# A hybrid DeltaNet / RWKV-7 step: the z projection of two segments moved out of the recurrence, with new pools, round order and job plan

## The chip, the cores and the metric

The kernel runs on one core of one Trainium2 chip. The metric is the device time of one execution in microseconds (us); lower is better. The kernel has five engines to schedule: TensorE (PE, matmuls; the load of a stationary operand is shown apart as PEld), VectorE (DVE), ScalarE (ACT), GpSimd (POOL) and SyncE (SP, which here issues every transfer).

## The reference

One step of a two-layer trunk over 1104 tokens: 64 sample tokens (8 sequences of 8) and 1040 prompt tokens (16 learned ones and 1024). Layer 0 is a gated DeltaNet and is not touched. Layer 1 is RWKV-7 time mixing. Cut to what the change touches:

```python
xx = xprev - xn
xs = xn[None] + xx[None] * mu[:, None, None, :]
rkvz = jnp.einsum('sbtd,sde->sbte', xs[:4], w_rkvz)      # four 1024x1024 projections
r, k, v, z = rkvz[0], rkvz[1], rkvz[2], rkvz[3]
...
def step(S, inp):                                         # per head of 64, 16 heads
    r_t, k_t, v_t, d_t, kk_t, b_t = inp
    S = (S * d_t[:, :, None, :]
         + jnp.einsum('bhvk,bhk->bhv', S, -kk_t)[..., None] * b_t[:, :, None, :]
         + v_t[..., None] * k_t[:, :, None, :])
    return S, jnp.einsum('bhvk,bhk->bhv', S, r_t)
...
y = (y - mean) * lax.rsqrt(var + GN_EPS) * lnx_w.reshape(H, N) + lnx_b.reshape(H, N)
y = y + jnp.sum(r_h * k_h * r_k, -1, keepdims=True) * v_h
y = y.reshape(B, T, D) * jax.nn.silu(z)
return y @ w_o, S, xn[:, -1]
```

After it come the residual add and a final RMSNorm.

## The kernel before

**Layout.** Activations lie with features on the partitions and tokens along the free axis. The tokens are cut into three segments (`SEGS`: 384, 384, 336). A product of a 1024-feature input with a 1024x1024 matrix is made in eight output tiles of 128 features; each fp32 product is three matmuls on split operands (high by high, low by high, high by low), so one output tile of one segment is 24 matmuls with 384 or 336 columns. `load_w` brings a tile's weights as two 256 KB transfers into `wraw` (two buffers) and splits them: ACT writes `whi`, POOL writes `wlo` (three buffers each).

**The dense stage of layer 1** (`layer1`). `keys_decay_rate` projects the keys and the decays. Then come the eight tiles of r (`todo` with m = 0) and the eight of v (m = 2), each over all three segments, by `project`. `mix` makes each projection's input from the normed activations `xb` into eight of eleven slots. Between the tiles stand five blocks of `rwkv_inverse`: each takes five (the last four) pair-segments through loads (`sld...`), a score product (`fL`), a chain of 31 steps on DVE (`inverse32`: `invtmp`, `invT`), a merge on PE (`mY`, `mU`) and a store of the result (`ttd`). They are started behind the tiles 1, 3, 5, 7 and 9. Then `mix_out` writes the mixed z input of segments 1 and 2 to HBM (`xzd`), and `gate_tiles` makes z of segment 0 (PSUM tile `dz`): per tile 24 matmuls, a tanh on ACT, a multiply on DVE and a store to `zd`. In this part a planner inside the framework orders every engine's instructions by its own simulated times, PE's too.

**The recurrence** (`wave`). There are 24 pair-segments: three segments by eight pairs of heads, each with six chunks of 64 tokens. The loop counts in half rounds `tau` from -3 to 53. Pair n starts at tau = 2n and makes one chunk each tau, so up to three pairs are in flight. `rwkv_front` prepares a pair (loads `fldcs`, `fldk`, `flda`, `fldr`, `fldv`; products on ACT, POOL and DVE) at tau = 2n - 3; its score products (`fG`), bonus (`fbonus`) and transposes (`fVT`, `fBT`) are dealt over the next two tau as `parts`. Each tau runs, for all pairs in flight:

1. `step_solve` and `step_scores` (matmuls into `rA`, then `X` on ACT),
2. `step_inner` (matmuls with `X`, then `UV` on ACT),
3. `step_state` (matmuls with `UV`, then the state `rS` on DVE).

Behind each of the three stages stand the parts, and then `fill`, which deals out dense work from a list `jobs`. At the end of the tau comes `step_outputs` (matmuls into `rA`, copied by ACT as `y`). PE's order is written out by hand here (`manual_schedule`); the planner orders the other engines. Two tau are one round, in which one pair begins and one ends. The end of a pair, `rwkv_finish`, normalises `y`, transposes it (`fyT`) and makes the operands `yh`, `yl` of the last product.

A job is a generator with a number of steps and a stretch of tau over which the steps are spread evenly; a step is six matmuls. The jobs before, in order: z of segment 1 (PSUM tile `zz`), the output product of segment 0 for pairs 0 to 3 (`project_out`, PSUM tile `zo`: eight tiles of 12 matmuls, added to `x1T` in HBM), the first half of z of segment 2, and so on; the final norms of segments 0 and 1 (`norms`: transposes `dfin`, then ACT, DVE, POOL) stand in the same list. `gates` reads its input back from `xzd`. The PSUM tiles of `zz` and `zo` have one buffer. Behind the loop come the output product of pairs 4 to 7 of segment 2 (96 matmuls into `d`) and the last norm.

**Pools.** Before the recurrence the pools of the dense stage are closed and `rwkv` and `fin` are opened from the right end of on-chip memory, where `xb` (8 tiles of 1113 floats, 35.6 KB per partition) lay outermost and the inverse's tiles further in. All of the recurrence's tiles are in `rwkv`, the masks and the states first.

Of the kernel before, what the change touches and what calls it, by code (L numbers as in the profile page):

```python
# [35 lines left out]
class Builder:  # L36
# [156 lines left out]
    def load_w(self, src, kt=8, into=None):  # L193
# [5 lines left out]
        for h in range(0, kt, 4):  # L199
            w = self.t(self.wp, [128, 4, 128], "wraw", 2)  # L200
            nc.sync.dma_start(w[:, :, 0:n], v[:, h:h + 4, :])
# [5 lines left out]
            self.split(w[:, :, 0:n], hi[:, :, 0:n], lo[:, :, 0:n], eng_lo="dve" if into else "pool")  # L207
# [800 lines left out]
    def mix(self, m, xb):  # L1008

        xs = [self.slots[(self.slot + k) % 11] for k in range(8)]  # L1010
        self.slot += 8
        for c0, n in SEGS:
# [4 lines left out]
    def mix_out(self, m, xb):  # L1017

        for k in range(8):
            for a, b in ((384, 768), (768, NT)):  # L1020
                x = self.mix_raw(m, k, a, b, xb[k], self.ev)
                self.nc.sync.dma_start(self.xzd[k][:, a:b], x)

    def gate_inputs(self, xa, s, pool, xb=None):

        nc, t = self.nc, self.t
        f = xa.rearrange("p k n -> p (k n)")[:, 0:6144].rearrange("p (x k n) -> p x k n", x=2, k=8)
        c0, n = SEGS[s]
        for k in range(8):
            if s == 0:  # L1030
                x = self.mix_raw(3, k, 0, n, xb[k], pool)
            else:
                x = t(pool, [128, 384], "zst", 2)[:, 0:n]
                nc.sync.dma_start(x, self.xzd[k][:, c0:c0 + n])
# [3 lines left out]
    def gate_tiles(self, x, s, ks, pool):  # L1038

        nc, t = self.nc, self.t  # L1040
        c0, n = SEGS[s]
        xh, xl = x
        load = lambda k: self.load_w(self.i["rwkv_w_rkvz"][0, 3][:, 128 * k:128 * k + 128])
        w = load(ks[0])
        yield
        for k in ks:
            w, w1 = load(k + 1) if k < ks[-1] else None, w
            p = self.ps("d", 4, "z") if s == 0 else self.ps("z", 1, "z")
# [8 lines left out]
            z = t(pool, [128, 384], "ev", 3) if s == 0 else t(pool, [128, 384], "zst", 2)  # L1057
            self.act(z[:, 0:n], p[:, 0:n], AF.Tanh, scale=0.5)
            nc.vector.scalar_tensor_tensor(z[:, 0:n], z[:, 0:n], 1.0, p[:, 0:n], op0=ALU.add, op1=ALU.mult)  # L1059
# [93 lines left out]
    def project(self, m, k, x, dst, apart=False):  # L1153
# [56 lines left out]
    def rwkv_masks(self, ap, first=False):  # L1210
# [22 lines left out]
        bones = t(ap, [128, 128], "pre", 3)  # L1233
# [12 lines left out]
    def rwkv_open(self):  # L1246
# [4 lines left out]
        self.xzd = self.dram([8, 128, NT], "xzd")  # L1251
# [79 lines left out]
    def rwkv_front(self, p, s):  # L1331

        nc, t, ap, col = self.nc, self.t, self.ap, self.pcol
# [11 lines left out]
        ld = self.rwkv_load(P.n, ap, "f", ("cs", "k", "a", "r", "v"))  # L1345
        kk, Dp, iD = self.rwkv_keys(p, ld, ap, "f")
        DC = P.DC = t(ap, [128, 14], "DC", NB + 2)
# [3 lines left out]
        AR = P.AR = t(ap, [128, 6, 2, 64], "AR", NB + 1)  # L1351
# [3 lines left out]
        k2 = t(ap, [128, 384], "k2", 1)  # L1355
# [4 lines left out]
        BK = t(ap, [128, 6, 2, 64], "BK", 2)  # L1360
# [4 lines left out]
        pr = t(ap, [128, 384], "pr", 1)  # L1365
        nc.vector.scalar_tensor_tensor(pr, ld["r"], pc("rwkv_r_k"), k2, op0=ALU.mult, op1=ALU.mult)
        ph, pl = t(ap, [128, 384], "prh", 1, F32R), t(ap, [128, 384], "prl", 1, F32R)
# [121 lines left out]
    def rwkv_finish(self, p, s, P):  # L1489
# [23 lines left out]
        t1 = t(ap, [128, 384], "k2", 1)  # L1513
# [68 lines left out]
    def project_out(self, s, yo, pairs, x2=None):  # L1582
# [6 lines left out]
        for ft in range(8):  # L1589
            if x2 is None:  # L1590
                x = t(self.fin, [128, 384], "zst", 2)
            elif len(x2) < 8:
                x = t(self.fin2, [128, 384], "x2", 8)
                x2.append(x)
            if x2 is None or pairs[0] == 0:
# [196 lines left out]
    def wave(self, xa, stay, last, pool):  # L1792
# [32 lines left out]
        def fill(now):  # L1825
            while jobs:
                f, k, a, b = jobs[0]
                if now < a:
                    return
# [75 lines left out]
```

## Time and profile before

| | us |
|---|---|
| three runs | 2449.97, 2446.77, 2454.0 (median 2449.97) |
| the profiled execution | 2446.91 |
| its span, first to last instruction of the program | 2445.1 |
| PE busy, share of the span | 2217.7, 91% |
| DVE, ACT, POOL busy | 1595.9, 1290.7, 1057.1 |
| mean granted clock of PE | 0.962 |

Positions are microseconds from the start of the span. The r projection starts at about 1472, the z tiles of segment 0 follow v at about 1770, and the first score product of the recurrence is at 1847.4. In a row of a stretch the columns are: the stretch, its length, then busy time and number of instructions of PE, PEld, DVE, ACT and POOL, the clock granted to PE as a share of full speed, the mean share of the DMA engines, and GB/s. In a row of waits stand who waited, for whom, the total, the number of times and the longest. Idle time of an engine that is not the bound costs nothing.

### The profile page before, as it was taken

The page shows a single profiled execution, that of the slowest core. Times are in us where ns is not written, and L with a number is a line of the kernel's source. Part 1 is how long each engine was busy: PE and PEld are TensorE (multiplying, and loading weights), DVE is VectorE, ACT ScalarE, POOL GpSimd, SP SyncE. Part 2 cuts the span into 40 slices and gives each one's busy share as a digit, 9 for nine tenths or more (in the row PEclk, how much of TensorE's full clock was granted, in tenths as well). Part 3 has the DMA queues.
Part 4 walks back from the last instruction along what each step waited for, and adds up shares of the span by engine and source line. Part 5 has one row for each costly group of instructions (what it writes and reads, how often), then busy time and mean ns, then how long its engine had stood idle before and what let it go on. Part 6 is the DMA issues. An engine that isn't in the chain of part 4 may idle for free. (4 is left out here: it accounts for less than half of the span.)

```text
span 2445.1 us, 54796 instructions
## 1 busy us (share of the span) xinstructions
PE 2217.7 (91%) x19737; PEld 1993.4 (82%) x19737; DVE 1595.9 (65%) x4193; ACT 1290.7 (53%) x3673; POOL 1057.1 (43%) x1454
## 2 busy tenths in 40 slices
PE   6989999999999999999999999988887898898887
PEld 5878989898888989889999998877775776777676
DVE  7878676876868595853357425698766675565554
ACT  5455555555656465564335557464334555555543
POOL 3435343433444344442314325453346556565534
PEclk9999999999999999999999999999987999999899
DMA  3323333333332424263441446767555345454542
GB/s 109 107 69 100 85 109 85 102 78 91 79 107 71 115 70 108 81 181 90 122 112 54 133 166 179 171 178 209 143 159 164 109 136 169 125 172 140 155 155 78
DMA packets 481546, 297.37 MB, mean 122 GB/s; under 512 B 188889, under 2 KB 466650, under 8 KB 481274
## 3 DMA queue, kind: packets, MB, share of 16 engines
q1 hardware_dynamic: 481274, 293.87, 42.7%
q8 instruction: 155, 2.54, 0.5%
q14 instruction: 117, 0.96, 0.1%
HBM read 206.30 MB, written 87.46 MB: 120 GB/s over the span
## 5 line engine op out<-in xcount | busy, mean ns | idle before, releaser
L90 POOL TENSOR_TENSOR wlo<-wraw,whi 128x512 fp32r<-128x512 f32 x260 | 346.1, 1333 | 418.6 <-ACT whi L86 392.2
L76 PE MATMUL d<-xc,whi 128*128 128x384 f32 (+3 forms) x846 | 236.5, 337 | 2.0 <-ACT ev L1160 2.0
L86 ACT CAST whi<-wraw 128x512 fp32r<-128x512 f32 x260 | 160.0, 616 | 138.6 <-PE dq L76 50.5
L410 DVE SCALAR_TENSOR_TENSOR cvy<-raw,cw,cvy 128x408 f32<-128x408 f32 (+2 forms) x288 | 178.0, 631 | 17.3 <-ACT cvy L62 15.4
L443 DVE TENSOR_TENSOR invtmp<-invA,invT 72x31 f32<-72x31 f32 (+31 forms) x403 | 164.5, 408 | 17.1 <-POOL invT L438 6.3
L445 DVE TENSOR_TENSOR invT<-invT,invtmp 72x31 f32<-72x31 f32 (+31 forms) x403 | 167.5, 416 | 6.3
L76 PEld LDWEIGHTS d<-xc,whi 128*128 128x128 f32 (+1 forms) x846 | 153.5, 188 | 9.6 <-issue 5.3
L76 PE MATMUL dz<-xc,whi 128*128 128x384 f32 (+1 forms) x480 | 149.3, 342 | 0.0
L76 PE MATMUL dv<-xc,whi 128*128 128x384 f32 (+1 forms) x480 | 146.8, 335 | 0.0
L76 PE MATMUL dz<-xa,whi 128*128 128x384 f32 (+1 forms) x416 | 141.1, 360 | 5.4 <-ACT whi L86 5.0
L76 PE MATMUL d<-xa,whi 128*128 128x384 f32 (+3 forms) x450 | 137.6, 339 | 3.4 <-ACT xa L86 2.5
L76 PE MATMUL d<-xc,wlo 128*128 128x384 f32 (+2 forms) x396 | 130.1, 338 | 0.0
L859 POOL TENSOR_SCALAR Sb<-Sb,eglb 128x128 f32<-128x128 f32 x128 | 79.6, 639 | 89.2 <-DMA Sb<-in_state_gdn 44.8
L76 PE MATMUL dv<-xa,whi 128*128 128x384 f32 (+1 forms) x288 | 99.9, 347 | 0.1
L76 PE MATMUL dz<-xa,wlo 128*128 128x384 f32 (+1 forms) x256 | 91.5, 358 | 0.9 <-POOL wlo L90 0.9
L76 PE MATMUL zz<-xa,whi 128*128 128x384 f32 (+1 forms) x256 | 84.8, 376 | 8.0 <-DVE zst L1059 8.0
L76 PEld LDWEIGHTS dz<-xc,whi 128*128 128x128 f32 x480 | 89.7, 192 | 0.8
L76 PEld LDWEIGHTS dz<-xa,whi 128*128 128x128 f32 x416 | 82.9, 201 | 8.6 <-ACT whi L86 6.8
L76 PEld LDWEIGHTS d<-xa,whi 128*128 128x128 f32 (+1 forms) x450 | 82.5, 188 | 8.3 <-ACT xa L86 2.8
L76 PEld LDWEIGHTS dv<-xc,whi 128*128 128x128 f32 x480 | 88.5, 188 | 0.5 <-issue 0.4
L76 PE MATMUL d<-xa,wlo 128*128 128x384 f32 (+3 forms) x252 | 85.1, 338 | 0.9 <-POOL wlo L90 0.9
L62 ACT ACTIVATE o<-rA,gcol 128x128 f32<-128x128 f32 x128 | 46.6, 371 | 74.5 <-DVE S L770 74.1
(512 smaller groups left out, 7119.7 us busy)
## 6 DMA issues: line engine op xcount, KB each, us to landing
wraw<-in_gdn_w_in SPq DMA_DIRECT2D x96, 256.0 KB
wraw<-in_rwkv_w_rkvz SPq DMA_DIRECT2D x96, 256.0 KB
Sb<-in_state_gdn SPq DMA_DIRECT2D x64, 256.0 KB
wraw<-in_rwkv_w_o SPq DMA_DIRECT2D x48, 256.0 KB
E<-drow SPq DMA_DIRECT2D x24, 384.0 KB
attn<-drow SPq DMA_DIRECT2D x24, 384.0 KB
wraw<-in_gdn_w_out SPq DMA_DIRECT2D x36, 256.0 KB
out_s_gdn<-Sb SPq DMA_DIRECT2D x32, 256.0 KB
```

The lines of the kernel that those rows point to most:

```text
L62: return self.nc.scalar.activation(out, in_, func, bias=bias, scale=scale, **kw)
L76: self.nc.tensor.matmul(out, lhsT, rhs, start=start, stop=stop)
L86: nc.scalar.copy(hi, x)
L90: e.tensor_tensor(lo, x, hi.bitcast(F32), op=ALU.subtract)
L410: nc.vector.scalar_tensor_tensor(y[:, 0:wd], raw[:, k:k + wd], cw[k], y[:, 0:wd], op0=ALU.mult, op1=ALU.add)
L443: nc.vector.tensor_tensor(tmp, A[:, j, j + 1:32].unsqueeze(2).broadcast_to([nb, n, m]), Tv[:, j, 0:m].unsqueeze(1).broadcast_to([nb, n, m] ...
L445: nc.vector.tensor_tensor(Tv[:, j + 1:32, 0:m], Tv[:, j + 1:32, 0:m], tmp, op=ALU.subtract)
L859: nc.gpsimd.tensor_scalar(Sb[:, u], Sb[:, u], self.eglb[:, hv, 4 * g + u:4 * g + u + 1], None, op0=ALU.mult)
```

## The change

- z of segments 0 and 1 becomes a third projection in the dense stage (`todo` has m = 3): `mix` puts its input in eight slots, and `project` makes two segments from each weight tile, with the tanh and the multiply (`gate`) where r and v have a copy. `mix_out` and the HBM buffer `xzd` go. The slots are given by a table.
- The input of segment 2 is made in the dense stage behind the first z tile (`gate_inputs` at n = 16), and only z of segment 2 is a job of the recurrence.
- The inverses start behind the tiles 1, 4, 7, 10 and 13 of 24.
- Pools: `front` (the tiles of `rwkv_front`) is opened first from the right, then `system` (masks, states, `UV`, `rTT`), then `rwkv` and `fin`.
- Round order: `step_outputs` follows `step_state` at once, and `fill` stands behind the second and the third stage, ahead of the parts; behind the first stage there is none.
- The job list: z of segment 2 over tau -2.5 to 14, then four output products of eight tau each with the PSUM tiles `z` (one buffer) and `d` (two) in turn, then segment 2. The norms are in a second list that runs beside it.
- The last product: pairs 4 to 6 over tau 52.1 to 54, and pair 7 alone behind the loop (24 matmuls). `load_w` takes fewer than four rows of tiles.

```diff
-        todo = [(m, k) for m in (0, 2) for k in range(8)]
+        todo = [(m, k) for m in (0, 2, 3) for k in range(8)]
+        slots = {0: (0, 1, 2, 3, 4, 5, 9, 10), 2: (6, 7, 8, 0, 1, 2, 9, 10), 3: range(3, 11)}
         for n, (m, k) in enumerate(todo):
             if k == 0:
-                x = self.mix(m, xb)
-            self.project(m, k, x, {0: self.rd, 2: self.vd}[m], k in range(8))
-            if n in (1, 3, 5, 7, 9):
-                self.rwkv_inverse((1, 3, 5, 7, 9).index(n), ip)
-        self.mix_out(3, xb)
-        for _ in self.gate_tiles(self.gate_inputs(xa, 0, self.ev, xb), 0, range(8), self.ev):
-            pass
+                x = self.mix(m, xb, slots[m], SEGS[0:2] if m == 3 else SEGS)
+            self.project(m, k, x, {0: self.rd, 2: self.vd, 3: self.zd}[m], k in range(8))
+            if n in (1, 4, 7, 10, 13):
+                self.rwkv_inverse((1, 4, 7, 10, 13).index(n), ip)
+            if n == 16:
+                zin = self.gate_inputs(xa, xb)
...
-        self.ap = rpool("rwkv", ctx)
-        fp = self.fin = rpool("fin", ctx)
-        self.rwkv_masks(self.ap)
-        t, ap = self.t, self.ap
+        self.fp, ap = rpool("front", ctx), rpool("system", ctx)
+        t, self.ap = self.t, rpool("rwkv", ctx)
+        self.fin = rpool("fin", ctx)
+        self.rwkv_masks(ap)
...
     def project(self, m, k, x, dst, apart=False):
...
-        ps = (self.dense(w, 128, *x, s, bufs=4) for s in range(3)) if apart else self.dense3(w, 128, *x)
+        ps = (self.dense(w, 128, *x, s, bufs=4) for s in range(2 if m == 3 else 3)) if apart else self.dense3(w, 128, *x)
         for (c0, n), p in zip(SEGS, ps):
             f = t(self.ev, [128, 384], "ev", 3)
-            nc.scalar.copy(f[:, 0:n], p[:, 0:n])
+            if m == 3:
+                self.gate(f[:, 0:n], p[:, 0:n])
+            else:
+                nc.scalar.copy(f[:, 0:n], p[:, 0:n])
             nc.sync.dma_start(dst[k][:, c0:c0 + n], f[:, 0:n])
...
-        ld = self.rwkv_load(P.n, ap, "f", ("cs", "k", "a", "r", "v"))
+        ld = self.rwkv_load(P.n, fp, "f", ("cs", "k", "a", "r", "v"))
     (and kk, Dp, iD, DC, AR, k2, BK, pr, prh, prl in fp likewise)
...
-            p = self.ps("z", 1, "o") if pairs[0] == 0 or s < 2 else self.ps("d", 2)
+            p = self.ps(*tag, "o")
...
-        jobs = [(lambda: gates(1, range(8)), 33, -3, 14), (lambda: out(0, 0), 17, 14, 19), (lambda: gates(2, range(4)), 20, 19, 24.5),
-                (lambda: out(0, 4), 17, 24.5, 30), (lambda: out(1, 0), 17, 30, 35), (lambda: gates(2, range(4, 8)), 17, 35, 40),
-                (lambda: norms(0), 11, 40, 41), (lambda: out(1, 4), 17, 41, 45), (lambda: norms(1), 11, 45, 47),
-                (lambda: out(2, 0, x2), 17, 47, 53.9), (lambda: out(2, 4, x2), 17, 54.1, 55), (lambda: self.finish(2, x2), 6, 55, 56)]
+        jobs = [(gates, 33, -2.5, 14), (lambda: out(0, 0, 4, Z), 17, 14, 22), (lambda: out(0, 4, 8, DD), 17, 22, 30),
+                (lambda: out(1, 0, 4, Z), 17, 30, 38), (lambda: out(1, 4, 8, DD), 17, 38, 46),
+                (lambda: out(2, 0, 4, Z), 17, 46, 51), (lambda: out(2, 4, 7, DD, x2), 17, 52.1, 54),
+                (lambda: out(2, 7, 8, DD, x2), 9, 54.1, 55), (lambda: self.finish(2, x2), 4, 55, 56)]
+
+        more = [(lambda: norms(0), 5, 31, 36), (lambda: norms(1), 5, 47, 51), (lambda: x2.extend(self.sums_in(2)) or iter(()), 1, 51.6, 52)]
...
-            stages = (self.step_solve, self.step_scores), (self.step_inner,), (self.step_state,)
+            stages = (self.step_solve, self.step_scores), (self.step_inner,), (self.step_state, self.step_outputs)
             for g in range(3):
                 for f in stages[g]:
                     for x in items:
                         f(*x)
+                if g:
+                    fill(tau + g / 2)
                 for f in parts[g]:
                     f()
...
-                fill(tau + (g + 1) / 3)
-            for x in items:
-                self.step_outputs(*x)
```

More of the change, by code (lines that the diff above doesn't have):

```diff
@@ L1006, in rwkv_norm, with mix @@
                 nc.sync.dma_start(self.o["p_rwkv_shift"][0][:, c], lr[9 * k + 8:9 * k + 9])
[L1008 to L1012, printed above, removed]
+    def mix(self, m, xb, slots, segs=SEGS):
+        xs = [self.slots[k] for k in slots]
+        for c0, n in segs:
             for k in range(8):
@@ L1331, in rwkv_front @@
     def rwkv_front(self, p, s):
-        nc, t, ap, col = self.nc, self.t, self.ap, self.pcol
+        nc, t, ap, fp, col = self.nc, self.t, self.ap, self.fp, self.pcol
         P = Ctx()
@@ L1648, in finish @@
                     nc.sync.dma_start(yp[128 * tt - 80:128 * tt - 80 + nr, hs], y[0:nr])
-            for _ in range(3 if s < 2 else 1):
-                yield
+            yield
     def build(self):
@@ L1786, in layer1 @@
         with tc.manual_schedule(engines={mybir.EngineType.PE}):
-            self.wave(xa, stay, last, pool)
+            self.wave(zin, stay, last, pool)
         last.close()
@@ L1790, in layer1, with wave, gates @@
         self.psum.close()
[L1792 removed]
+    def wave(self, zin, stay, last, pool):
         nc, t = self.nc, self.t
         P, x2 = {}, []
[L1798 to L1813 removed]
+        Z, DD = ("z", 1), ("d", 2)
+        out = lambda s, a, b, tag, x=None: self.project_out(s, [P[8 * s + q].out for q in range(a, b)], range(a, b), tag, x)
+        def gates():
+            yield from self.gate_tiles(zin)
+            stay.close()
+            self.fin2 = pool("fin2", last)
+            self.fw = t(self.fin2, [128, D], "fw")
+            nc.sync.dma_start(self.fw, self.i["final_norm_w"].rearrange("(o d) -> o d", o=1).broadcast_to([128, D]))
+        def norms(s):
             x = self.sums_in(s)
```

112 lines of the change are left out of this document (44 added, 68 removed).

## The prediction

> **What bounds the kernel now.** I read the page first (who is busy, where the clock drops), then the stretches of layer 1 one by one, then PE's waits in each of them, then the chain that ended last.
>
> ```profile
> PE 2217.7 (91%) x19737; PEld 1993.4 (82%) x19737; DVE 1595.9 (65%) x4193; ACT 1290.7 (53%) x3673; POOL 1057.1 (43%) x1454
> PEclk9999999999999999999999999999987999999899
> ```
>
> PE is the busiest by far, and its clock dips at three quarters of the span, where the dense stage of layer 1 hands over to the recurrence. So the question is what PE does per stretch. I cut layer 1 at the start of the recurrence (1847.4) and at the transposes `fyT` of pairs 0, 3, 19 and 22, that is at the ends of tau 7, 13, 45 and 51:
>
> ```profile
> 1472.00:1770.00 298.00, 269.24 (x2572) 233.50 (x2571) 224.16 (x484) 162.61 (x351) 124.52 (x191) 0.97 0.67 176
> 1770.00:1847.40 77.40, 52.85 (x546) 45.54 (x545) 51.28 (x100) 30.15 (x63) 38.54 (x61) 0.79 0.64 178
> 1847.40:1941.80 94.40, 84.22 (x897) 68.71 (x897) 53.70 (x141) 48.72 (x129) 54.33 (x74) 0.89 0.43 124
> 1941.80:2004.00 62.20, 55.14 (x773) 44.16 (x771) 43.83 (x129) 35.16 (x105) 34.75 (x42) 1.00 0.46 128
> 2004.00:2366.10 362.10, 311.65 (x3863) 261.76 (x3859) 204.04 (x600) 200.90 (x623) 202.35 (x220) 0.93 0.51 151
> 2366.10:2404.80 38.70, 33.49 (x447) 27.31 (x445) 21.57 (x80) 17.72 (x64) 19.14 (x19) 0.99 0.37 111
> 2404.80:2445.10 40.30, 24.63 (x197) 22.64 (x194) 17.36 (x42) 10.38 (x25) 16.80 (x16) 0.92 0.26 81
> ```
>
> In these rows no other engine is above 76% of a stretch, and PE's idle time (length less busy) plus what the low clock costs is the whole room: idle 28.8 + 24.6 + 10.2 + 7.1 + 50.5 + 5.2 + 15.7 = 142 us, and the clock (1 less its share, times the length) 9 + 16 + 10 + 0 + 25 + 0 + 3 = 63 us. The change adds and removes hardly any matmul; it can only win or lose in these 200 us.
>
> **The change part by part.**
>
> The price of a matmul: in a stretch where PE never stops,
>
> ```profile
> 1400.00:1450.00 50.00, 50.00 (x301) 50.00 (x300) 11.27 (x12) 21.82 (x42) 9.66 (x11) 1.00 0.48 167
> ```
>
> 301 of them take 50 us, 0.166 us each at full clock. Now the fill, one row of tile `zz`, then two of tile `zo`:
>
> ```profile
> 2004.00:2366.10 362.10, 40.42 (x192) 32.76 (x192) 3.98 (x8) 3.58 (x8) 0.93 0.51 151
> 2004.00:2366.10 362.10, 85.63 (x384) 67.18 (x384) 17.59 (x32) 0.93 0.51 151
> 2366.10:2404.80 38.70, 14.30 (x72) 10.97 (x72) 2.68 (x6) 0.99 0.37 111
> ```
>
> *z moved.* 192 matmuls of segment 1 go from the recurrence to the dense stage: 192 x 0.166 = 32 us off the one, 32 us onto the other. z of segment 2 takes the place that segment 1 had at the start (same steps per tau), so the 192 of tau 14 to 45 are what vanishes from the recurrence. With the tile go 8 weight tiles less (16 transfers, 16 casts on ACT, 16 subtractions on POOL) and 32 transfers of `xzd`; none was on PE's path except in the handover, so I cost them at nothing there. The mixing of z is the same 24 pieces as before; the tanh and multiply of eight more tiles come to the dense stage beside 8.0 us of PE work per weight tile.
>
> *Dense stage, r and v (298 us).* Same PE work. The inverses start every 3 tiles in place of every 2. PE's waits here are theirs:
>
> ```profile
> PE fL L76 <- DVE skk L1305: 10.2, 10, 2.6
> PE fbpp L73 <- DMA invR<-rssd: 7.0, 3, 3.3
> ```
>
> DVE is at 224 of 298 us, so a thinner stream should lose less; the slots 9 and 10, read last by the keys, may cost r's first tile 1 to 2 us. I take -5, between -15 and +15.
>
> *Handover (77.4 us).* Now:
>
> ```profile
> PE fG L76 <- POOL fDp L1270: 13.6, 1, 13.6
> PE dz L76 <- ACT whi L86: 5.0, 6, 1.7
> 1830.22 1.17 PE L76 MATMUL mU<-sTT,invY 32*32 32x32 f32 x24 [0.43 <-DMA sTT<-r_u]
> 1834.06 0.32 SPq L1328 DMA_DIRECT2D ttd<-sTT  x1
> 1836.98 0.50 SPq L1261 DMA_DIRECT2D fldcs<-csd  x1
> 1847.44 1.65 PE L76 MATMUL fG<-AR,BK 64*128 64x128 f32 x12 [13.64 <-POOL fDp L1270]
> ```
>
> The last inverse stores its result at 1834.06; only 2.9 us later the first load of the recurrence (`fldcs`) is issued, SP's queue having stood before that behind weights and z input; then loads, ACT, POOL and DVE of one whole front run before `fG`, with PE idle for 13.64 us. After the change the front's tiles (seven loads and three keys of 1.5 KB, AR 15.4, BK 6.1 and the rest, 43 KB a partition) lie mostly on the 35.6 KB of `xb`, whose last reader is the input of segment 2 behind the first of eight z tiles. So the first fronts can run under seven tiles of z, and one weight tile now feeds 48 matmuls (8.0 us) where it fed 24 (4.0 us), against 5.0 us of weight waits now. The new stretch is 384 x 0.166 = 64 us for z, the rest of the inverses' matmuls (546 - 186 = 360, at 1.17 us per 24 at half clock, so 0.024 each at full: 9 us), and 5 for stops: 78 us, +1. Bounds: 73 with no stop, 96 if the whole hole and the weight waits stay. What would be late next is the last inverse: it starts behind tile 13, about 1472 + 14/16 x 295 = 1730, and its PE work stands ahead of the recurrence. I count on it ending inside the z tiles.
>
> *Tau -2 to 13 (94.4 + 62.2 us).* Same fill. The first stretch now starts with a cold clock (0.89 of 94.4 us: 10 us lost) and 10 us idle; with fronts ready and PE coming straight from z I take half: -9 (0 to -15), and -2 for the next.
>
> *Tau 14 to 45 (362.1 us, sixteen rounds of 22.6).* The first and the last of three quiet rounds, then the `zo` work of the first, then PE's waits over the stretch:
>
> ```profile
> 2139.60:2159.30 19.70, 18.30 (x241) 15.37 (x239) 12.18 (x37) 12.21 (x38) 12.64 (x14) 1.00 0.60 173
> 2179.30:2198.80 19.50, 18.05 (x243) 15.28 (x239) 12.27 (x37) 11.92 (x38) 12.68 (x14) 1.00 0.58 169
> 2139.60:2159.30 19.70, 7.81 (x36) 6.09 (x36) 1.60 (x4) 1.00 0.60 173
> PE rA L80 <- ACT y L1487: 12.5, 15, 1.7
> PE zo L76 <- DVE zst L1610: 11.9, 9, 2.5
> PE dfin L73 <- DVE f2k L1643: 7.9, 3, 3.6
> PE zz L76 <- DVE zst L1059: 7.2, 4, 3.4
> PE fG L76 <- DVE k L1514: 1.1, 1, 1.1
> ```
>
> A quiet round is 19.7 us with 36 fill matmuls and PE busy 18.1. After the change four output products of 96 are spread over these sixteen rounds: 24 a round. 19.7 - 12 x 0.166 = 17.7. The wait for `y` goes, since `step_outputs` now has fill and parts behind it before its PSUM tile is wanted: 12.5 us over 16 rounds, but not all of it in quiet ones, so -0.5: 17.2 a round. The 22.6 of today is the quiet round plus bursts: up to 48 fill matmuls in a round, two steps on a one-buffer tile in a row (the waits on `zst`), the norms' eleven steps in one tau (`dfin`), and the low clock behind each. In the new list a one-buffer tile has about five us between its steps, and the norms take five tau. So 16 x 17.2 = 275, plus 8 for sample rows and the 48 `dfin` transposes, plus 10 for stops that I can't place: 293, -69. Bounds: PE's bare work, (18.1 - 2.0) x 16 + 8 = 266; and all of today's stops kept, 362 - 32 = 330.
>
> Three waits could take the place of those removed. `X` now has only the score products between `step_scores` and `step_inner`:
>
> ```profile
> 2161.24 0.72 ACT L62 ACTIVATE X<-rA,rk 128x64 f32<-128x64 f32 x3 [1.46 <-PE rA L80]
> 2161.35 1.10 PE L76 MATMUL fG<-AR,BK 64*128 64x128 f32 x12
> ```
>
> All three `X` end at 2161.96, the score products at 2162.45: covered, so I cost it at nothing; if ACT is late with them by the length of one of its other instructions in half of the tau, that is 0.3 us a tau, 10 us, inside the bounds. `UV` and `rS` keep a fill step and a part ahead of their readers. On SP the norms' `x1T` loads now stand among the weights of the running product; at five tau apiece they have time.
>
> *Tau 46 to 51.* 96 fill matmuls in place of 72, 24 x 0.161 = +4, norms(1) there too, less stops: +4.
>
> *The end (40.3 us).* The transpose of pair 23, then the chain that ended last:
>
> ```profile
> 2412.20 0.92 PE L76 MATMUL fyT<-ident,y 64*64 64x64 f32 x24 [1.69 <-POOL y L1507]
> 2415.87 6.12 PE d L76 x38
> 2423.34 2.83 DMA wraw<-in_rwkv_w_o
> 2426.27 0.63 ACT whi L86
> 2426.97 1.29 POOL wlo L90
> 2430.70 0.67 PE dfin L73 x4
> ```
>
> 38 matmuls in 6.12 us are 0.161 each. Now pair 23's output waits 7.4 us (2404.8 to 2412.2), 96 matmuls and stops take 17.5, the last norm 15. After: 72 matmuls (11.6) stand ahead of the transpose of pair 23, then about 3 us of DVE, ACT and POOL for `yh` and `yl` with nothing on PE to cover them, then 24 matmuls (3.9) fed by eight small weight tiles through two `wraw` buffers. A 256 KB tile now takes 2.83 + 0.63 + 1.29 us from transfer to `wlo`; a quarter of it I put at 2.7, 1.35 per tile with two buffers, so some 7 us. Then 15. Together 11.6 + 1 + 3 + 7 + 15 = 38 with no stop; I take 41, +1 (-3 to +6).
>
> Sum: -5 + 1 - 9 - 2 - 69 + 4 + 1 = -79 on the profiled span of 2445.1: 2366. That execution was 2446.91, 1.8 above its span, and 3.1 below the median 2449.97; so 2366 + 5 = 2371.
>
> On the clock, the row of the handover has 0.79 over 77.4 us, 16 us lost around one hole of 13.6. The Trainium skill, "TensorE: Matmul & The Clock Gate", section "What's actually happening", says PE falls to half rate after an idle window of about 3.4 us and comes back after one busy window; that hole would then cost 1.7 us and not 16, and waits under 3.4 us nothing. By that rule the clock's share of my gain in tau 14 to 45 would be near zero and the sum some 15 us worse; the row of that stretch (0.93 of 362 us, 25 us lost, with longest waits of 3.6 us) speaks against taking it so strictly.
>
> **The rivals.**
>
> *The rounds are paced by DVE and POOL, not by PE.* In the quiet rounds each is busy 12.2 to 12.7 of 19.7 us, and a front is a chain over ACT, POOL and DVE on single buffers. For it: VectorE's products with POOL beside them are stretched,
>
> ```profile
> L1366 DVE SCALAR_TENSOR_TENSOR pr<-fldr,pcol,k x24: 604/636/1616, 1845.2 to 2325.9; 128x384 f32<-128x384 f32 x24
> ```
>
> 0.60 us at best and 1.62 at worst, and shorter rounds put more of them beside each other. Against it: PE's waits for the front in tau 14 to 45 are 1.1 us in all (`fG`). If it holds, rounds stay at 19.5: 16 x 2.3 = 37 us more, 2408. The Trainium skill, "GPSIMD Engine Reference", section "1. Specifications", says that POOL shares VectorE's ports to on-chip memory when VectorE has two inputs there, which fits the row; it does not say how much.
>
> *The hole stays.* The pools do not do what the layout allows: the last inverse, started later, or SP's queue holds the first front to the end of z. Then 13.6 us idle and the cold start (8) come back: 2393.
>
> *Slower: the recurrence does not shorten at all.* The dense stage takes its 32 us for z of segment 1, while a round is a latency chain (state to solve to inner to state) that fill only pads, so that less fill is only more idle time. Then 2450 + 32 = 2482 less the handover's gain of up to 20. Its point: a round of tau 14 to 45 must fall from 22.6 by 2.0 us to pay for the 32 us; at over 20.6 the change loses. Against it:
>
> ```profile
> 2381.00:2393.40 12.40, 5.96 (x30) 4.57 (x30) 1.13 (x3) 1.00 0.24 68
> ```
>
> Two tau with two pairs in flight and 30 fill matmuls took 12.4 us, so the chain is no longer than about 6 us a tau, against 8.6 forecast.
>
> **How the numbers follow.** Forecast (2335 to 2400): 0.64. Paced by DVE and POOL (about 2408): 0.13. The hole stays, or the stops of today stay in part, up to 2430: 0.12. The recurrence does not shorten: 0.07. Between them, within 0.3% (7 us, about what three runs can tell from no change): 0.04. The range takes in the first two and the better half of the third, 2335 to 2425: the low end is -79 with the bounds of the recurrence (266 for 293) and a little of the dense stage; the high end is the stops kept (330 for 293) with the hole half kept. Faster 0.89, same 0.04, slower 0.07.
>
> **What would show it.** Right: `fG` follows the last z matmul of the dense stage within 3 us, near 1848; the rounds of tau 14 to 45 are near 17 to 18 us with PE over 90% busy; the wait of `rA` for `y` is gone from PE's list; the stretch after the last round is about as long as now. Wrong: a wait of `rA` on `X` of some us in all, `fG` waiting for the front, PE waiting for `mU` of the last inverse at the end of z, or the last weight tiles late by more than 10 us.

## The result, and the profile after

| | before | after |
|---|---|---|
| median of the runs | 2448.37 us | 2420.19 us (2414.01 to 2422.7) |
| ratio to before | | 0.9878, 95% interval 0.9851 to 0.9905 |
| profiled execution | 2446.91, span 2445.1 | 2422.7, span 2421.0 |

The kernel is 28 us faster in the medians and 24 in the profiled pair. The forecast was 79: the sign was right, the size was not. The page's row of PE, its clock, and then the stretches of layer 1 (columns as before), cut at the first `fG` and at `fyT` of pairs 0, 3, 19 and 22:

```profile
PE 2213.4 (91%) x19737; PEld 2003.7 (83%) x19737; DVE 1620.5 (67%) x4201; ACT 1279.8 (53%) x3665; POOL 1049.8 (43%) x1446
PEclk9999999999999999999999999999998999999998
```

```profile
1472.00:1770.00 298.00, 273.69 (x2532) 237.35 (x2531) 220.32 (x471) 162.09 (x351) 127.15 (x195) 0.95 0.64 164
1770.00:1860.50 90.50, 80.30 (x776) 74.80 (x774) 61.50 (x124) 38.37 (x81) 43.93 (x62) 0.94 0.49 142
1860.50:1957.60 97.10, 81.55 (x897) 68.55 (x899) 57.86 (x148) 47.65 (x128) 54.78 (x74) 0.91 0.46 131
1957.60:2026.80 69.20, 58.30 (x785) 49.06 (x782) 47.62 (x130) 34.83 (x106) 37.75 (x44) 0.93 0.41 115
2026.80:2329.40 302.60, 269.23 (x3659) 232.20 (x3653) 211.99 (x583) 180.26 (x582) 178.38 (x199) 0.97 0.52 155
2329.40:2377.90 48.50, 39.78 (x484) 32.57 (x483) 25.55 (x83) 21.56 (x72) 22.90 (x23) 1.00 0.52 163
2377.90:2421.00 43.10, 25.33 (x174) 21.81 (x170) 18.71 (x47) 10.65 (x30) 15.15 (x21) 0.84 0.26 80
```

| stretch | before | forecast | after | miss |
|---|---|---|---|---|
| r, v, handover, to the first `fG` | 375.4 | 371 | 388.5 | +17 |
| up to tau 7 | 94.4 | 85 | 97.1 | +12 |
| tau 8 to 13 | 62.2 | 60 | 69.2 | +9 |
| tau 14 to 45 | 362.1 | 293 | 302.6 | +9.5 |
| tau 46 to 51 | 38.7 | 43 | 48.5 | +6 |
| end | 40.3 | 41 | 43.1 | +2 |

Six misses of one sign add up to 55 us (79 less the 24 of this pair); the rounds did shorten from 22.6 to 18.9 us. A first clue is in the page: DVE is busy 25 us longer than before, with eight instructions more. PE's waits in tau 14 to 45:

```profile
PE rA L80 <- ACT X L62: 15.9, 11, 1.6
PE rA L80 <- DVE rS L1470: 12.7, 29, 2.2
PE rA L80 <- ACT y L1481: 2.4, 5, 1.4
```

The waits on `zst` and `dfin` are gone and `y` is down from 12.5. In their place stand two that I had costed at nothing: `X`, and `rS`. Here is one place of the first, from the timeline (start, length, instruction, idle time before it and what ended it):

```profile
2142.51 1.69 DVE L1509 SCALAR_TENSOR_TENSOR lz<-k,lnb,lz 128x384 f32<-128x384 f32 x1
...
2142.53 1.26 POOL L90 TENSOR_TENSOR wlo<-wraw,whi 128x512 fp32r<-128x512 f32 x1
...
2142.41 0.52 ACT L62 ACTIVATE X<-rA,rk 128x64 f32<-128x64 f32 x2 [1.33 <-PE rA L80]
2144.24 0.51 ACT L86 CAST yh<-lz 128x384 fp32r<-128x384 f32 x1 [1.31 <-DVE lz L1509]
2144.66 0.70 ACT L62 ACTIVATE k<-flda,omka,pcol 128x384 f32<-128x384 f32 x1
2145.27 0.29 ACT L62 ACTIVATE X<-rA,rk 128x64 f32<-128x64 f32 x1
...
2145.62 0.45 PE L80 MATMUL rA<-X,rTT 128*64 128x64 f32 x4 [1.54 <-ACT X L62]
```

Two `X` are made at once. The third stands in ScalarE's queue behind `yh` and `k`, and both wait for VectorE's `lz`: `yh` reads it, and `k` writes the tile `k2`, in which `lz` still reads the first product of the finished pair. `lz` itself takes 1.69 us, with POOL's `wlo` beside it to 2143.79. In 13 of the 16 rounds `lz` takes 1.4 us or more, and there it ends about 0.4 us behind a POOL instruction that started with it (`wlo` in 12 of them); in the other three `wlo` had ended 0.05 us after the start of `lz`, and `lz` took about 0.6. The group of `lz` in tau 14 to 45 (ns, least, median and most), first before, then after:

```profile
L1515 DVE SCALAR_TENSOR_TENSOR lz<-k,lnb,lz x16: 546/616/687, 2006.3 to 2345.3; 128x384 f32<-128x384 f32 x13, 128x336 f32<-128x336 f32 x3
```

```profile
L1509 DVE SCALAR_TENSOR_TENSOR lz<-k,lnb,lz x16: 556/1692/1698, 2028.8 to 2315.0; 128x384 f32<-128x384 f32 x13, 128x336 f32<-128x336 f32 x3
```

The Trainium skill, "SBUF — State Buffer", section "Who interferes with whom", says that a VectorE instruction with two inputs in on-chip memory contends with a POOL instruction that reads it, for a port pair that is an exclusive lock, and that the order of issue decides who blocks. The trace fits: `lz` ends 0.41 us behind `wlo`, at 2144.20, as if it had waited for it. Their starts are 0.02 us apart, so which was issued first can't be read here.

### The profile page after: what moved, and what is told of

It is laid out like the page before. It is cut to its first block, busy times and chain, and to the rows that moved or that the text cites. A ratio compares the mean times of both kernels' runs of the same rounds, so it can differ in the third digit from the quotient of the medians.

```text
span 2421.0 us, 54809 instructions
## 1 busy us (share of the span) xinstructions
PE 2213.4 (91%) x19737; PEld 2003.7 (83%) x19737; DVE 1620.5 (67%) x4201; ACT 1279.8 (53%) x3665; POOL 1049.8 (43%) x1446
## 5 line engine op out<-in xcount | busy, mean ns | idle before, releaser
L90 POOL TENSOR_TENSOR wlo<-wraw,whi 128x512 fp32r<-128x512 f32 (+2 forms) x252 | 331.8, 1319 | 379.9 <-ACT whi L86 361.6
L76 PE MATMUL d<-xc,whi 128*128 128x384 f32 (+2 forms) x910 | 258.3, 341 | 4.5 <-POOL xc L90 2.5
L86 ACT CAST whi<-wraw 128x512 fp32r<-128x512 f32 (+2 forms) x252 | 152.0, 605 | 145.4 <-PE dq L76 50.7
L76 PEld LDWEIGHTS d<-xc,whi 128*128 128x128 f32 (+1 forms) x910 | 167.5, 191 | 10.7 <-issue 3.4
L76 PE MATMUL d<-xc,wlo 128*128 128x384 f32 (+2 forms) x428 | 142.3, 341 | 1.4 <-POOL wlo L90 1.4
L76 PE MATMUL dz<-xa,whi 128*128 128x384 f32 (+1 forms) x288 | 100.1, 348 | 0.0
L80 PE MATMUL rA<-UV,G 128*64 128x64 f32 x1152 | 63.6, 240 | 26.0 <-DVE rS L1470 24.0
L76 PE MATMUL d<-xh,wlo 128*128 128x384 f32 (+1 forms) x256 | 84.1, 344 | 1.5 <-POOL wlo L90 1.5
L76 PE MATMUL d<-xh,whi 128*128 128x384 f32 (+1 forms) x256 | 84.2, 344 | 0.7 <-ACT whi L86 0.4
```

The lines of the kernel that those rows point to most:

```text
L76: self.nc.tensor.matmul(out, lhsT, rhs, start=start, stop=stop)
L80: self.nc.tensor.matmul(out, lhsT, rhs, start=start, stop=True, skip_group_check=True)
L86: nc.scalar.copy(hi, x)
L90: e.tensor_tensor(lo, x, hi.bitcast(F32), op=ALU.subtract)
```

## The experiments

Each is an edit of the changed kernel, unless it says otherwise. They ran on four chips on which the kernel before takes 2438 to 2439 us, where it took 2448 beside the change; what is compared is each one's ratio to the kernel before on its own chip, beside the 0.9878 of the change. Stretches are those of its profiled execution, cut at the same marks. Theory 1 at the start was: the new order leaves `X` and `rS` without fill ahead of their readers.

**Where fill and outputs stand.** Four kernels change this part of a tau (`fill_three` has the first line alone, `outputs_behind_fill` all, `two_slots_outputs_behind` the two slots of the change and the outputs):

```diff
-                if g:
-                    fill(tau + g / 2)
+                fill(tau + (g + 1) / 3)
+                if g == 2:
+                    for x in items:
+                        self.step_outputs(*x)
                 for f in parts[g]:
```

> The changed kernel with its dense plan in three slots again, so that a slice of fill also stands behind the score products, ahead of the inner products that read X; the outputs stay right behind the state. Theory 1 (the missing cover): PE's wait for X in the rounds, 15.9 us in 11 places of 302.6 us, goes to under 4, the rounds' clock stays at 0.97 or above, and the 302.6 us fall by 8 to 15: 2405 to 2412 us in all. Rival (the round is a latency chain): the fill that covers X is missing behind the inner and the state products, PE waits for UV and rS instead, the sum of the waits stays within 5 us, and the time stays at 2415 to 2425.

Measured: 0.9882 (0.9863 to 0.9901), no gain. `X` fell to 6.7 us, but `rS` grew to 16.7, and PE now waits 12.3 us for VectorE's `G` ahead of `fbonus`; the rounds are 308.4. That is the rival's form: a cover taken from one place is missed in another. Tau 8 to 13 (64.7 for 69.2) and 46 to 51 (43.7 for 48.5) gained what the rounds lost.

> The changed kernel with the whole round order of before: outputs at the end of a tau, the parts ahead of three slots of fill. Layout, z, dense plan and last product stay changed. Theory 1: the waits for X (15.9 us) and for rS (12.7 us in 29 places) go, the wait for y (2.4 us now, 12.5 us in the kernel before) returns: the rounds' 302.6 us fall by 5 to 15, 2405 to 2415 us. Rival (the new order is what shortens the rounds, and z and the plan give little): the rounds go back towards 320 and the time to 2435 or more.

Measured: 0.9895 (0.987 to 0.9921). `X` and `rS` are down to 0.4 and 2.7 us and `lz` to 0.61 us, but `y` costs 29.5. The rounds are longer, 315.7, and tau 8 to 13 (59.9 for 69.2) and 46 to 51 (41.2 for 48.5) shorter. In sum the round order of the change was worth nothing beside the even plan.

> The changed kernel with three slots of fill, and the outputs moved behind the last slot: state, fill, outputs, parts. So X, UV and rS each have a slice of fill ahead of their reader. Theory 1: X and rS are both down to under 4 us in the rounds, y stays under 4, and the time falls by 12 to 22: 2398 to 2408 us, more than with the three slots alone. Rival (the round is a latency chain): the waits move to UV or to the front and the time stays at 2415 to 2425.

(The outputs are taken out of the stage of `step_state`, too.) Measured: 0.979 (0.9766 to 0.9815), rounds 292.5: against `fill_three` the outputs' place is worth 22 us. `rS` is down to 6.5 us and `X` to 1.1.

> The changed kernel with its two slots of fill as they are, and only the outputs moved: state, fill, outputs, parts. X still has no fill ahead of its readers. Theory 1 in its narrow form (the outputs right behind the state, waiting for VectorE's read of the same PSUM tile, are most of the loss in the rounds): rS in tau 14 to 45 from 12.7 us to under 7, X stays at 12 to 18, a ratio of 0.979 to 0.983. Theory 1 in its wide form (both covers are wanted together): 0.983 to 0.986. Rival (the wait moves on to y, now late again): 0.987 or more.

Measured: 0.9746 (0.9729 to 0.9763), some 32 us below the change, more than with three slots. Tau 8 to 13 and tau 14 to 45:

```profile
1951.90:2010.10 58.20, 54.25 (x785) 45.16 (x783) 43.07 (x128) 32.54 (x100) 37.84 (x42) 1.00 0.51 142
2010.10:2294.80 284.70, 263.47 (x3659) 222.30 (x3654) 194.98 (x586) 181.01 (x589) 176.16 (x201) 0.98 0.54 166
```

```profile
PE rA L80 <- ACT y L1481: 14.0, 14, 2.7
PE fG L76 <- DVE k L1508: 3.4, 3, 1.8
PE rA L80 <- ACT X L62: 2.7, 9, 0.9
PE rA L80 <- DVE rS L1470: 0.8, 1, 0.8
```

`X` went with `rS`, though it has no fill ahead of it here. So theory 1 was wrong for `X`: a cover is not what it lacked. What changed for it is `lz`, 0.62 us again, as the order of VectorE and POOL moved against each other.

**What makes X late.** Two edits at the second half of a pair's finish, alone and together:

```diff
-        t1 = t(self.fp, [128, 384], "k2", 1)
+        t1 = t(self.fin, [128, 384], "lt1", 1)
...
-        self.split(zg[:, 0:n], yh[:, 0:n], yl[:, 0:n])
+        self.split(zg[:, 0:n], yh[:, 0:n], yl[:, 0:n], "dve")
```

> The changed kernel with one cast moved: yh of a finished pair is written by VectorE, which wrote its input, in place of ScalarE, in whose queue it stands ahead of X. The round order is untouched. If X is late because its queue is held by that cast: PE's wait for X falls from 15.9 us to under 6 and the time by 5 to 12, to 2408 to 2415 us. If X is late because a latency chain without cover is seen whatever the queue holds: the wait stays above 12 us. If VectorE's pace is the limit: 24 casts of some 0.5 us more on it lengthen the rounds by up to 12 us.

(The second edit alone.) Measured: 0.9878 (0.9857 to 0.9899), nothing. `X` is 13.0 us: `k` alone now holds the queue, 20.2 us of ScalarE's waits for `lz`, and `lz` is still 1.70 us.

> The changed kernel with two edits that free ScalarE's queue ahead of the third X: the first product of a finished pair gets a tile of its own (it shared k2 with the next front's k, so that k waited for lz), and yh is cast by VectorE. The outputs stay right behind the state. If X is late because its queue stands behind yh and k, which wait for VectorE's lz: X in tau 14 to 45 goes from 15.9 us to under 4. If X carries the loss, the rounds fall from 302.6 to 285 to 290, a ratio of 0.980 to 0.983; if the outputs' wait for rS carries it, rS stays at 12 to 20 us, the rounds at 295 to 303, a ratio of 0.985 to 0.989.

(Both.) Measured: 0.979 (0.9767 to 0.9812). `X` 4.7 us, `rS` 9.3 in 31 places, the rounds 278.5. Here `lz` is still stretched (median 1.09 us): once nothing ahead of `X` waits for it, that costs PE little.

> The changed kernel with one edit: the first product of a finished pair gets a tile of its own in place of k2; yh stays on ScalarE. If the shared tile alone makes X late (k waits for lz): X in tau 14 to 45 under 6 us, the rounds at 278 to 285, a ratio of 0.978 to 0.982. If yh, which waits for lz too, holds the queue as long as k did: X stays at 12 to 16 us, the rounds at 297 to 303, 0.985 to 0.989.

(The first alone.) Measured: 0.9775 (0.976 to 0.979). Tau 14 to 45, its waits, and `lz`:

```profile
2020.80:2296.40 275.60, 259.23 (x3659) 224.54 (x3653) 199.65 (x581) 177.77 (x581) 174.67 (x199) 1.00 0.56 168
```

```profile
PE rA L80 <- DVE rS L1470: 9.6, 32, 0.6
PE rA L80 <- ACT X L62: 3.4, 7, 0.7
```

```profile
L1509 DVE SCALAR_TENSOR_TENSOR lz<-lt,lnb,lz x16: 553/606/1648, 2023.7 to 2282.0; 128x384 f32<-128x384 f32 x13, 128x336 f32<-128x336 f32 x3
```

One tile of 1.5 KB gives 27 us in the rounds, 17.2 each, the forecast's figure. With it the order of the queues moved too (in one round that I read, `k` goes ahead of the first `X`, `yh` behind the third, and `lz` no longer meets `wlo`; in 6 of the 16 rounds `lz` still takes 1.62 us or more), so the tile is shown as the lever, and which of these three does how much is not.

**Freed and outputs together**, with the last product whole:

> The changed kernel with the own tile, yh on VectorE, the outputs behind the second slot of fill and the last product whole. If X freed and outputs moved take away different waits: the rounds at 275 to 280, tau 8 to 13 at 58 to 60, a ratio of 0.967 to 0.971. If they take away the same wait: the rounds at 282 to 286, 0.972 to 0.976, as outputs_and_whole (0.973).

```profile
1958.20:2018.50 60.30, 54.78 (x783) 45.51 (x781) 47.05 (x133) 33.56 (x104) 39.24 (x44) 0.97 0.45 129
2018.50:2289.40 270.90, 261.01 (x3657) 220.75 (x3651) 202.64 (x598) 173.25 (x567) 185.82 (x199) 0.99 0.56 171
```

Measured: 0.9721 (0.9702 to 0.9739). The rounds fell to 270.9, so the waits are partly different ones; the whole is not told apart from `outputs_and_whole` (below). Both are faster than the kernel before and than the changed one.

**What z, the plan and the last product are worth.**

```diff
-        (lambda: out(0, 0, 4, Z), 17, 14, 22), (lambda: out(0, 4, 8, DD), 17, 22, 30),
-        (lambda: out(1, 0, 4, Z), 17, 30, 38), (lambda: out(1, 4, 8, DD), 17, 38, 46),
+        (lambda: out(0, 0, 4, Z), 17, 14, 19), (lambda: out(0, 4, 8, Z), 17, 24.5, 30),
+        (lambda: out(1, 0, 4, Z), 17, 30, 35), (lambda: norms(0), 5, 40, 41), (lambda: out(1, 4, 8, Z), 17, 41, 45),
```

(`norms(0)` leaves the second list.)

> The changed kernel with the windows of before for the four output products of segments 0 and 1 (tau 14 to 19, 24.5 to 30, 30.5 to 35, 41.5 to 45), all on the one-buffer tile, and norms(0) in one tau of the same list. z, the layout, the round order and the last product stay changed. If the even plan is what the forecast took it for (bursts cost a wait on a one-buffer tile and a low clock behind each), tau 14 to 45 goes from 302.6 to 318 to 328 us, a ratio of 0.994 to 0.998. Rival (what counts is the 192 matmuls that left; quiet rounds give back what bursts take): within 5 us, 0.986 to 0.990.

```profile
2011.00:2357.00 346.00, 283.59 (x3659) 240.92 (x3653) 204.08 (x578) 182.16 (x581) 176.84 (x198) 0.90 0.46 138
```

Measured: 1.0059 (1.004 to 1.0079), slower than the kernel before. In the rounds the same matmuls take 43 us longer than 302.6: 62.4 us of PE idle for 33.4, and the clock at 0.90.

`z_alone` adds to this plan the round order of before and the last product whole:

> The changed kernel with its round order, its dense plan up to tau 46 and its last product all as before; what stays of the change is z of two segments in the dense stage, the pools, and the loads of the last sums. By the forecast's terms (32 us off the recurrence, 32 us onto the dense stage, starts and handover a little better, bursts kept): 2440 to 2450, a ratio of 0.996 to 1.000. Theory from the bursts' run (1.006): moving z alone loses, as the dense stage pays 32 us and more for what the rounds, paced by bursts and covers, give back only in part: 1.003 to 1.010.

Measured: 0.9953 (0.9931 to 0.9975), rounds 331.2: near what the forecast's terms give, and the theory from the bursts' run was wrong. With the old round order the bursts cost 15.5 us in the rounds (331.2 for the 315.7 of `order_undone`), with the new one 43. So the even plan and the round order can't be priced apart from each other; why the old order bears bursts better was not tried further.

> The kernel before with one edit: in each stage the slot of fill stands ahead of the parts, and the outputs go behind the third slot, ahead of the parts, in place of the end of the tau. z, plan and last product are as before. If the wait for y (12.5 us in its rounds) and what follows from it on the clock is a cost of the order alone: 10 to 20 us, a ratio of 0.992 to 0.996. Rival (with bursts and one-buffer tiles the rounds are bound by those): 0.997 to 1.002.

(The kernel before with fill ahead of the parts and the outputs behind the third slot.) Measured: 0.9948 (0.9927 to 0.9968): `y` fell from 12.5 to 2.8 us and the rounds from 362.1 to 351.3. This order helps on its own, by 13 us; it is not the order of the change.

> The changed kernel with the last product undone: pairs 4 to 7 of segment 2 as one product of 96 matmuls behind the loop, as in the kernel before; the loads of x for it stay early. Theory 1 (the split ties PE to four small weight tiles and to yh and yl with nothing beside them, so it gives little): the end is within 3 us of now, tau 46 to 51 as now, a ratio of 0.986 to 0.989. Rival (72 matmuls ahead of the last pair's transpose are a clear gain): the time is 6 to 10 us longer, 0.990 to 0.992.

```diff
-                (lambda: out(2, 4, 7, DD, x2), 17, 52.1, 54), (lambda: out(2, 7, 8, DD, x2), 9, 54.1, 55), ...
+                (lambda: out(2, 4, 8, DD, x2), 17, 54.1, 55), ...
```

Measured: 0.9865 (0.9844 to 0.9885), the end 38.7 us for 43.1, tau 46 to 51 as in the changed kernel (49.1 for 48.5). Splitting the product off cost 4 us.

> Two slots with the outputs behind the second, and the last product whole behind the loop. If the end's 4 us add to the best so far (0.9746): 0.972 to 0.974. Rival (within the scatter): 0.975 to 0.977.

Measured: 0.973 (0.9707 to 0.9753), end 39.2: the 4 us show in the trace and are near the scatter in the time.

**The handover.** `front_on_xb` has these lines (and `ld["v"]` in `ap`):

```diff
-        pr = t(fp, [128, 384], "pr", 1)
-        ph, pl = t(fp, [128, 384], "prh", 1, F32R), t(fp, [128, 384], "prl", 1, F32R)
+        pr = t(ap, [128, 384], "pr", 1)
+        ph, pl = t(ap, [128, 384], "prh", 1, F32R), t(ap, [128, 384], "prl", 1, F32R)
```

> The changed kernel with four tiles of the front (fldv, pr, prh, prl: 7.7 KB a partition) moved to the pool rwkv, so that the rest of the pool front, 35.7 KB, lies on xb alone; no instruction is added or taken away. In the changed kernel 7.6 KB of that pool lie on the inverse's tiles, and its first loads stand in SP's queue behind the last inverse's last store. Theory 1 (the place of that pool holds the first fronts): the first loads go out some 20 us earlier, fG follows the last z matmul at once, in place of 3.2 us, and the stretch up to tau 7, 97 us with 15.5 us idle, falls to 85 to 90: 8 to 14 us off the whole, a ratio to the kernel before of 0.982 to 0.985 where the changed kernel has 0.988. Rival (the masks and zeroed tiles, still on the inverse's place, hold the start as long): under 3 us, 0.987 or more.

First the changed kernel, then this one:

```profile
1847.38 0.32 SPq L1322 DMA_DIRECT2D ttd<-sTT  x1
1848.20 0.38 SPq L202 DMA_DIRECT2D wraw<-in_rwkv_w_rkvz  x1
1848.63 0.49 SPq L1255 DMA_DIRECT2D fldcs<-csd  x1
...
1860.53 1.42 PE L76 MATMUL fG<-AR,BK 64*128 64x128 f32 x12 [3.19 <-POOL BK L1356]
```

```profile
1785.11 0.50 SPq L1255 DMA_DIRECT2D fldcs<-csd  x1
...
1848.82 0.94 PE L76 MATMUL fG<-AR,BK 64*128 64x128 f32 x12 [1.39 <-DVE BK L1355]
```

The first half of the theory held: with the pool on `xb` alone the loads go out 64 us ahead of `fG`, where they stood behind the last inverse's store, 12 us ahead. The second did not: 0.9905 (0.9881 to 0.993), no gain, and up to tau 7 100.3 us. The late front was a visible wait, and not what the stretch costs.

```diff
-            if n in (1, 4, 7, 10, 13):
+            if n in (1, 3, 5, 7, 9):
```

> The changed kernel with the five inverses begun behind tiles 1, 3, 5, 7 and 9 again in place of 1, 4, 7, 10 and 13. By the forecast (a thinner stream loses 5 us less of PE in the dense stage, but its end is late): dense stage and z from 380 to 383 to 388 us, the last inverse ends 8 us or more sooner, a ratio of 0.987 to 0.991. Rival (the inverses' own chain sets their pace, whenever they begin): the last inverse ends within 3 us of where it ends now, the stretch stays at 378 to 382 us, 0.986 to 0.989.

Measured: 0.9863 (0.9847 to 0.9879). From r's first store to `fG` 378.7 us, where the other kernels with z in the dense stage have 376.5 to 382.7; on that scale the last inverse ends at 364.9 us, 3.9 sooner than in the changed kernel, but kernels with the later start have 362.5 to 370. So starting sooner does nothing that shows, as the rival said; that the inverses' own chain sets their pace fits this and is not shown by it.

**Combinations.** Three slots, the outputs behind, the front on `xb`, and the end of the last product held back (`all_three`, the diff; the last norm moves from tau 55 to 56) or whole (`three_and_whole`); `outputs_whole_front` is `outputs_and_whole` with the front on `xb`.

```diff
-        (lambda: out(2, 4, 7, DD, x2), 17, 52.1, 54), (lambda: out(2, 7, 8, DD, x2), 9, 54.1, 55), ...
+        (lambda: out(2, 4, 7, DD, x2), 17, 52.1, 55.5), (lambda: out(2, 7, 8, DD, x2), 9, 55.6, 56), ...
```

> The front on xb alone, the outputs behind the last of three slots of fill, and the last 33 matmuls of the product of pairs 4 to 6 held back behind the transpose of pair 23, to cover yh and yl. If the three act in different stretches, as theory 1 has it, their gains add: 20 us by the outputs (measured, 0.979), 8 to 14 by the front, 2 to 4 by the end: a ratio of 0.964 to 0.970. Rival (what one takes off shows up as a wait elsewhere): 0.975 to 0.980.

> A candidate to beat both: three slots with the outputs behind the last, the front on xb alone, the last product whole behind the loop. From the runs: 0.979 with the outputs, less 4 us of the end (38.7 for 42.9), less 0 to 5 us of the start: a ratio of 0.975 to 0.978. Rival (these gains are within what runs of one kernel scatter): 0.979 to 0.981.

> The same and the front on xb alone. If the first fronts are worth 4 us once the round order doesn't stall (88 to 89 us up to tau 7 in two kernels, 93 to 97 without): 0.970 to 0.973. Rival (as in the changed kernel, where it gave nothing): as the run without it, 0.972 to 0.976.

Measured: 0.9791 (0.9767 to 0.9816), 0.9763 (0.9743 to 0.9784) and 0.9784 (0.9762 to 0.9807). The gains don't add: the first equals the outputs alone, and the last is worse than without the front (97 us up to tau 7 for 91). Moving the first loads among the z tiles gave 4 us there with three slots and took 3 to 6 with two; why was not found.

## Why the forecast was right in sign and too large

The sign came from the right bound. The size failed where waits were put at nothing or taken to go. Of the 55 us, 17 stand in the dense stage with the handover and 12 in the stretch up to tau 7, where the stops did not go as forecast; 9 in tau 8 to 13, where `rS` was put at nothing; and in the rounds `X`, put at nothing, costs 27, of which a margin hides 18. The first sign of being wrong that the prediction lists, a wait of `rA` on `X`, came. The 2420 lie in that part of its range which it keeps for today's stops staying.

- **Bound and direction.** PE's stops were the room, and the even plan took the bursts out: right. `bursts_again` shows it as 43 us of the rounds, but beside the old round order it is 15.5. z alone, forecast at about nothing, is 0.5%.
- **Tau 14 to 45, -69 forecast, -59.5 measured.** The failed term is `X`: "covered, so I cost it at nothing", with at worst "the length of one of its other instructions", 10 us. It is two other instructions, both waiting for a third on VectorE that a neighbour on POOL had stretched to 1.69 us, and freeing it gave 27 us. That the total missed by 9.5 only is luck: the 18 us that I added for sample rows, `dfin` and stops were not needed (without the wait the rounds are 275.6, where 275 stood in the sum ahead of them). 17.2 a round was the right figure for a kernel without this wait (275.6 / 16).
- **`rS`.** "`UV` and `rS` keep a fill step and a part ahead of their readers" is wrong as a reading of the code. `step_outputs` follows `step_state` at once and writes the PSUM tile that VectorE is reading for `rS`; all 29 waits for `rS` in the changed kernel's rounds stand there. Putting a slot of fill between them takes tau 8 to 13 from 69.2 to between 58.2 and 61.1 in the four kernels with two slots, where the forecast had 60.
- **r, v and handover, +1 and -5 forecast, +13 measured.** The hole did shrink from 13.6 to 3.2 us, not for the reason given: part of the pool lay on the inverse's tiles, and its first load was issued just behind the last inverse's store, as the rival of the hole had it; what covered the loads is z. What failed is the claim that the stops would go with the hole. Idle plus clock over 1472 to `fG` went from 78 to 55 us (rows above, by the same sum as in the forecast), and the two terms needed 42 (78 - 4 - 32 of z). In r and v alone the idle time did fall about as forecast, from 28.8 to 24.3 us, but the clock fell from 0.97 to 0.95, 6 us more by that sum, so nothing was won there. (The sum counts the low clock also where PE stood idle: of the handover's 16 us before, 9 fell on PE's work.) The longest waits left are the inverses' own:

```profile
PE fL L76 <- DVE skk L1299: 11.0, 5, 3.4
PE mY L76 <- DMA T1n<-r_t: 4.7, 3, 4.1
PE mY L76 <- issue: 2.7, 1, 2.7
```

  Neither the front's place nor sooner inverses moved that stretch; how to shorten it stays open.
- **Up to tau 7, -9 forecast, +2.7 measured.** I halved the cold clock because fronts would be ready. With the loads 64 us early the stretch was 100.3, so that reason falls. The clock did not recover (0.91 for 0.89), and 10 of the 15.5 us of idle time are waits for `X` and `rS`, which had no term here either:

```profile
PE rA L80 <- DVE X L1440: 4.0, 1, 4.0
PE rA L80 <- DVE rS L1470: 3.2, 6, 0.8
PE rA L80 <- ACT X L62: 1.9, 1, 1.9
PE rA L80 <- DVE rS L1468: 1.3, 2, 0.9
```

  The stretch was 88 to 100 in all variants, and which of its parts sets that was not settled.
- **Tau 46 to 51, +4 forecast, +10 measured.** 47 to 50 us in the kernels with two slots, 41 to 45 with three: here the two-slot fill costs some 5 us that I had no term for.
- **The end, +1 forecast, +3 measured.** The last transpose came 16.9 us behind the one of pair 22, where the forecast had 11.6 + 1 for the 72 matmuls between; undoing the split gave 38.7.
- **The rivals.** "Paced by DVE and POOL" was near the truth in its row, a product of VectorE stretched to 1.6 us beside POOL, and wrong in its mechanism: not their pace, but one such instruction ahead of others in a queue. The hole did not stay, though the first load was as late as that rival said; a round fell by 3.7 us, past the 2.0 at which the change pays.

## What to carry to other kernels

Before costing a wait at nothing, list what stands ahead of the producer in its engine's queue and what those wait for: an unrelated scratch tile with one buffer, used by two stages, was worth 27 us. Put independent PE work between an instruction that lets another engine read a PSUM tile and the next one that writes that tile. And what moving work off a loop pays depends on how the rest is spread and in which order: the same 192 matmuls less went with a gain of 1.0 to 1.2% with an even plan in either round order, and with bursts with a gain of 0.5% in the old order and a loss of 0.6% in the new one.

## What the runs showed of the hardware that I had not expected

The granted clock changes on a grid of 3.41 us. I cut layer 1 of all twenty traces on it and counted, for each stretch at full clock, whether the next was at half. With PE idle for under 0.8 us in all in the 3.41 none of 3978 was; between 0.8 and 1.5 us 49 of 486; between 1.5 and 1.9 113 of 164; above 1.9 us all of 202 but one, which had 1.90. So a single wait of 1.5 us that falls into one stretch is at the edge, and a half stretch in which PE is busy throughout costs 1.7 us. Of the five half stretches in the changed kernel's rounds four come right behind a wait for `X` of 1.54 or 1.55 us, the fifth behind one for `rS` of 1.53; `yh_on_vector` shortened the wait for `X` to 1.27 at most and had no half stretch there, with more idle time in all (37.8 us for 33.4). The Trainium skill, "TensorE: Matmul & The Clock Gate", section "What's actually happening", gives the free-running window of about 3.4 us, which the grid bears out; it asks for an idle window before the clock halves, and here 1.5 us of idle time, under half a window, was often enough. So the forecast did well not to take waits under 3.4 us as free on the clock.
